# Experts' weights loaded in 8 KB runs, four tiles a step, with a seventh weight buffer

## The chip, the core and the metric

The kernel runs on one core of a Trainium2 chip. The metric is the device time of one execution in microseconds (us). The profile used here is of one further execution of the same program. Engines are named as in the profile: PE is the tensor engine's matmul, PEld its weight load, DVE the vector engine, ACT the scalar engine, POOL GpSimd, and SP the engine that issues nearly all loads, in the order of its program.

## What is computed

The network has two blocks, all in float32, for 256 tokens of 1024 features. The first block has two layers: attention with forget gates and then a mixture of experts; retention and then another mixture of experts. The second block, also of two layers, mixes tokens and a context of 256 rows (mLSTM, a gating unit, a convolution) and has dense feed-forward halves. The change lies in the mixture of experts, which is this:

```python
def hier_moe(h, wr_g, br_g, wr_e, br_e, w_gu, w_down):
    ...                                   # group of 8 experts by top-1, two experts in it by top-2
    return grouped_experts(xf, expert_id, gates, w_gu, w_down)

def grouped_experts(xf, expert_id, gates, w_gu, w_down):
    ...                                   # each token's row goes to its two experts e
    a, b = jnp.split(xb @ w_gu[e], 2, axis=-1)
    return (jax.nn.silu(a) * b) @ w_down[e]
    ...                                   # rows weighted by their gates, summed per token
```

There are 32 experts in each of the two layers. `w_gu[e]` is 1024 x 1024 (512 columns of gate, 512 of up; 4 MB), `w_down[e]` is 512 x 1024 (2 MB). So one layer reads 192 MB of experts' weights for 256 tokens.

## The kernel before

**Phases.** Attention runs from 0 to about 195 us of the profile, layer 0's experts from there to 760, retention to about 980, layer 1's experts from about 1000 to 1620, and the second block's own tail follows to the end. The second block's work on the context does not depend on the first block, so it is woven into the experts: `moe` is a generator that yields after each step, and at each yield the caller advances the *side work* by 0.8 of a step in layer 0 (the context's mixer, until about 607 us) and 0.88 in layer 1 (its feed-forward, then a mixer again). In layer 0 the experts run alone from there to 760 us.

**Experts.** A layer goes through eight groups q of four experts. Each expert has 32 places for tokens; the four experts' places are 128 rows of the products, and expert j uses columns 32 j to 32 j + 31 of the PE array, so four matmuls stand side by side. `gather(q)` (L895) puts the tokens of a group into `xg`, features on partitions, by products with the one-hot array `oh`; L173/`affine` multiplies by the gain column of each 128 features. The gate/up products (L956) go through eight chunks k of 128 features; each chunk has two halves of 512 columns and four experts: eight matmuls. Then ACT takes the silu (L965), DVE multiplies (L966), PE transposes the result `ha` (L969) into `hT`, and the down products (L976) go through four chunks k of 128 inner units, again eight matmuls each. A step, from yield to yield, is two chunks: sixteen matmuls. After the first two chunks of the down products the next group's gather and the transposes of its gates (`placed`, L923) are written; the result of group q - 1 is brought to the tokens (`combine`, L986) after chunk 3 of group q's gate/up products.

**Weights.** All large weights, the side work's too, go through tiles of 1 MB ([128, 2048] float32) from one pool `wp` of six places, taken in turn by `wt` (L126): a tile gets the place of the sixth tile before it, as soon as all its reads are done. At a layer's start three further places (`e0` to `e2`) are used first. Experts' tiles are loaded by `wload2` (L153), side weights by `wload` (L137), all issued by SP in program order; a load whose place is still in use holds up every load behind it. `pair(q, k)` loads chunk k of the four experts as two tiles of two experts: each partition holds one row of 1024 floats (4 KB) of each expert. So a chunk needs two tiles, and after its eight matmuls both are free. Group 7's down weights are loaded otherwise, in four quarters of the columns (1 KB runs, 0.5 MB each).

**The order around it.** At layer 0's start SP issues the first gate/up tiles, then small rows for the second block, and a load of the largest count of tokens per expert into a register (`cnti`, L1024). Before group 7 there is a branch on that count: an expert with more than 32 tokens would be computed densely there (`overflow`). The scheduler orders each engine's instructions by data dependence and program order; the sums over features are accumulated in PSUM.

Of the kernel before, what the change touches and what calls it, by code (L numbers as in the profile page):

```python
# [19 lines left out]
NEG = -1e30  # L20
RS = -8192.0                    # what rsqrt's scaled form carries
NE, CAP, FF = 32, 32, 512
R0, R1, R2, R3, R4 = 1.8, 0.8, 1.0, 0.88, 0.7           # steps of other work per step of the main path
AHEAD = 200                     # instructions that what the others wait for goes ahead of
TAPS = 6                        # convolution taps between other work
PIECE, WS = 512, 6              # elements per partition split at a time; pieces on chip
# [3 lines left out]
# columns of the constant array  # L30
C_ID, C_LE, C_LT, C_GE, C_ONE = 0, 128, 256, 384, 512
C_Z, C_LOW, C_UP = 640, 768, 896          # 0 where col <= row / col >= row, else NEG
C_IOTA, C_GRP, C_I8 = 1024, 1056, 1088
C_SEL, C_OFF = 1096, 1112                 # row 32 j + i, column i; rows of scales: what to add, 1 / RS
C_COS, C_SIN, C_RET = 1116, 1372, 1628         # rotary, decay
NCST = C_RET + 4 * 384

# modulation vectors: which third of the columns of w_mod, and which two of its quarters
# [4 lines left out]
def constants():  # L43
    """Tables that depend on shapes alone."""
# [35 lines left out]
class Tags:  # L80
    """A pool, some of whose tags lie in another one under other names."""
# [10 lines left out]
class Net:  # L92
    def __init__(self, tc, I, out, es):
# [8 lines left out]
        self.flip, self.extra = 0, []  # L102
        self.later, self.pending, self.taken = [], [], False
        self.early, self.hold = -99, None                  # pieces of weights whose low parts GpSimd makes

# [7 lines left out]
    def bank(self):  # L113
        """One bank, from the other pool while g's are taken."""
        return self.m()[:, 0:512] if self.taken else self.g()

    def two(self, mode, apart=False):
        """Two banks."""
# [7 lines left out]
    def wt(self, name):  # L126
        """A weight tile; some lie in the places of tiles that are no longer needed."""
        if self.extra:
            return self.pre.tile([P, 2048], F32, tag=self.extra.pop(0), name=name)
        return self.wp.tile([P, 2048], F32, tag="w", name=name)  # L130

    def wload(self, src):
        """One tile of weights: rows (k p) of src on the partitions."""
# [6 lines left out]
    def wtile(self):  # L140
        """A weight tile as [P, 2, D]."""
        return self.wt("w").rearrange("p (b d) -> p b d", b=2)

    def gain(self, src, g):
        """src [D] on all partitions."""
# [3 lines left out]
    def wload2(self, src):  # L149
        """The same rows of two experts: src [2, P, 1024]."""  # L150
        w = self.wt("w")
        v = w.rearrange("p (e c) -> p e c", e=2)
        self.nc.sync.dma_start(v, src.rearrange("e p c -> p e c"))  # L153
# [13 lines left out]
    def affine(self, o, i, scale, bias=None, eng=None):  # L167
        """o = i * scale + bias, per partition."""
# [10 lines left out]
    def split(self, pool, tag, src, shape=None, low=None):  # L179
        """src = H + L exactly, both in the tensor engine's one-pass format."""  # L180
# [12 lines left out]
    def wparts(self, w, mode):  # L193
        """Parts of a weight tile [P, k, c]: each a function of (row block, first column, last column)."""
# [15 lines left out]
    def pairs(self, a, b):  # L210
        """Products that make up a.b for operands in parts."""
        return [(a[0], b[0])] if len(a) == 1 else [(a[0], b[0]), (a[1], b[0]), (a[0], b[1])]

    def rstd(self, ss, n, eps=EPS):
        """1/sqrt(ss/n + eps)"""
# [4 lines left out]
    def rsqrt(self, h, scaled=False):  # L220
        """1/sqrt(h): a first guess from the exponent's bits, then Newton's steps. Scaled: RS times it, for one column."""
# [9 lines left out]
        for _ in range(3):  # L231
            if scaled:                  # y = c / sqrt(h) to (y h y - 3 c c) y = -2 c^3 / sqrt(h)
# [13 lines left out]
    def rms(self, x, b, junk, act=False):  # L246
        """rstd of token block b of x [P, 2, D]"""
# [12 lines left out]
    def transposed(self, xn, b, cb):  # L260
        """cb(k, psum [P, n, 128]) for the feature chunks k .. k + n of token block b of xn [P, 2, D]"""
# [1576 lines left out]
```

## Time and profile before

| | us |
|---|---|
| median of three runs | 2349.8 |
| the runs | 2347.91, 2349.8, 2354.22 |
| span of the profiled execution, first to last instruction | 2346.0 |
| what lies around the span, against the median | 3.8 |
| PE busy in the span | 2127.2 (91%) |
| VectorE busy | 1060.9 (45%) |
| mean granted clock of TensorE, share of full speed | 0.970 |
| loaded in the span | 686.64 MB, mean 293 GB/s |

The page divides the span into forty slices of 58.65 us and gives for each the busy tenths of each engine and of the DMA engines, PE's granted clock and the rate of transfer. The other views are of stretches of the span: busy time of each engine with the clock and the share of time in which the DMA engines were moving (the table by stretch), waits by what ended them, the queue's packets, and single instructions in order of time. The shares of a stretch are worth more here than those of the span, since phases have different limits.

### The profile page before, as it was taken

To read this page: it belongs to the slowest core of one execution; us is meant where nothing else is said; L and a number is where in the kernel's file an instruction comes from. 1 tells how busy PE (TensorE), PEld (TensorE's weight loads), DVE (VectorE), ACT (ScalarE), POOL (GpSimd) and SP (SyncE) were. 2 spreads that over 40 slices of the span, in tenths; PEclk is the share of its full clock that TensorE was granted. 3 is DMA by queue.
4 is the path that set the end of the run, shared out by engine and by line. 5 is a ranking of instruction groups with operands and counts; after the bars stand their busy time and mean duration, and the time that the engine had idled before them with its cause. 6 is when DMAs were issued, how large, how long until landed. Compare 5 with 4: busy or idle time off the path is not lost. (4 is left out here: it accounts for less than half of the span.)

```text
span 2346.0 us, 32803 instructions
## 1 busy us (share of the span) xinstructions
PE 2127.2 (91%) x12844; PEld 1433.4 (61%) x12845; DVE 1060.9 (45%) x2513; ACT 695.6 (30%) x1420; POOL 172.9 (7%) x194
## 2 busy tenths in 40 slices
PE   8998899889877999989899999987998998998998
PEld 7765445344222776855444444334787997787997
DVE  6556053322101766531121221415778556777555
ACT  4353111211000434520000000012555554554554
POOL 1001000000000111010000000001212002102000
PEclk9999999999988999989999999999999999999999
DMA  8864999999999977579999999999756554555551
GB/s 257 313 245 166 350 399 392 369 399 378 379 409 384 323 281 246 203 268 382 391 398 393 399 390 390 367 356 346 256 162 202 188 190 156 187 181 171 192 185 63
DMA packets 305320, 686.64 MB, mean 293 GB/s; under 512 B 22056, under 2 KB 163784, under 8 KB 298888
## 3 DMA queue, kind: packets, MB, share of 16 engines
q1 hardware_dynamic: 305096, 684.45, 79.9%
q8 instruction: 103, 1.69, 0.3%
q14 instruction: 57, 0.47, 0.1%
q10 hardware_dynamic: 64, 0.03, 0.0%
HBM read 681.78 MB, written 2.62 MB: 292 GB/s over the span
## 5 line engine op out<-in xcount | busy, mean ns | idle before, releaser
L190 DVE TENSOR_TENSOR wl<-w,wh 128x512 fp32r<-128x512 f32 x574 | 396.3, 707 | 252.4 <-ACT wh L185 233.7
L185 ACT CAST wh<-w 128x512 fp32r<-128x512 f32 x600 | 364.3, 621 | 355.5 <-PE psm L430 111.6
L956 PE MATMUL psm<-w,xg 128*32 128x512 f32 x2048 | 319.8, 632 | 61.8 <-DMA w<-in_expert_w_gu_dram 55.0
L430 PE MATMUL psg<-xt,w 128*128 128x256 f32 x1056 | 235.8, 381 | 20.5 <-DMA w<-in_w_gu_dram 11.3
L430 PEld LDWEIGHTS psg<-xt,w 128*128 128x128 f32 x1056 | 198.0, 190 | 71.1 <-issue 38.6
L956 PEld LDWEIGHTS psm<-w,xg 128*32 128x32 f32 x2048 | 66.4, 112 | 270.6 <-issue 150.4
L430 PE MATMUL psg<-xh,wh 128*128 128x256 f32 x608 | 177.2, 291 | 3.9 <-ACT wh L185 2.4
L430 PE MATMUL psm<-xh,wh 128*128 128x256 f32 x640 | 179.9, 281 | 0.6 <-ACT ffh L1450 0.6
L430 PE MATMUL psm<-xh,wl 128*128 128x256 f32 x640 | 179.8, 281 | 0.0
L430 PE MATMUL psm<-xl,wh 128*128 128x256 f32 x640 | 179.7, 281 | 0.0
L430 PE MATMUL psg<-xh,wl 128*128 128x256 f32 x608 | 175.1, 288 | 2.4 <-DVE wl L190 2.4
L430 PE MATMUL psg<-xl,wh 128*128 128x256 f32 x608 | 173.8, 286 | 0.0
L976 PE MATMUL psm<-w,hT 128*32 128x512 f32 (+1 forms) x1152 | 156.7, 564 | 16.0 <-DMA w<-in_expert_w_down_dram 12.5
L430 PEld LDWEIGHTS psg<-xh,wh 128*128 128x128 f32 x608 | 118.1, 194 | 18.6 <-ACT wh L185 9.5
L430 PEld LDWEIGHTS psm<-xh,wh 128*128 128x128 f32 x640 | 120.7, 189 | 1.9 <-ACT ffh L1450 1.1
L430 PEld LDWEIGHTS psm<-xh,wl 128*128 128x128 f32 x640 | 120.6, 188 | 0.7
L430 PEld LDWEIGHTS psg<-xh,wl 128*128 128x128 f32 x608 | 118.0, 194 | 4.9 <-DVE wl L190 4.2
L430 PEld LDWEIGHTS psm<-xl,wh 128*128 128x128 f32 x640 | 120.8, 189 | 0.0
L430 PEld LDWEIGHTS psg<-xl,wh 128*128 128x128 f32 x608 | 117.9, 194 | 0.3 <-issue 0.2
L965 ACT ACTIVATE ha<-psm 128x512 f32<-128x512 f32 x16 | 9.6, 597 | 334.3 <-PE psm L956 334.3
L988 DVE TENSOR_TENSOR x<-x,psg 128x512 f32<-128x512 f32 (+1 forms) x72 | 45.1, 628 | 123.2 <-PE psg L986 123.0
L976 PEld LDWEIGHTS psm<-w,hT 128*32 128x32 f32 x1152 | 38.6, 111 | 93.2 <-issue 52.2
(497 smaller groups left out, 3263.9 us busy)
## 6 DMA issues: line engine op xcount, KB each, us to landing
w<-in_expert_w_gu_dram SPq DMA_DIRECT2D x256, 1024.0 KB
w<-in_expert_w_down_dram SPq DMA_DIRECT2D x112, 1024.0 KB
w<-in_w_gu_dram SPq DMA_DIRECT2D x66, 1024.0 KB
w<-in_w_mod_dram SPq DMA_DIRECT2D x48, 1024.0 KB
w<-in_w_in_dram SPq DMA_DIRECT2D x40, 1024.0 KB
w<-in_w_down_dram SPq DMA_DIRECT2D x33, 1024.0 KB
w<-in_ret_w_in_dram SPq DMA_DIRECT2D x24, 1024.0 KB
w<-in_fox_w_in_dram SPq DMA_DIRECT2D x16, 1024.0 KB
```

Source lines behind the costliest of these rows:

```text
L185: nc.scalar.copy(h, src)
L190: eng.tensor_tensor(l, src, h.bitcast(F32), op=ALU.subtract)
L430: self.nc.tensor.matmul(o, a, x, start=i == 0, stop=i == len(mm) - 1)
L956: nc.tensor.matmul(gu[32 * j:32 * j + 32, half * 512:(half + 1) * 512], xg[:, k, 32 * j:32 * j + 32], ws[j // 2][:, j % 2, half * 512:(hal ...
L965: nc.scalar.activation(ha, gu[:, 0:512], AF.Silu)
L976: nc.tensor.matmul(o[32 * j:32 * j + 32, :], hT[:, k, 32 * j:32 * j + 32], w(j), start=k == 0, stop=k == 3)
L988: v.tensor_tensor(o, o, ps, op=ALU.add)
```

## The change

`wload2` loads 256 rows of one expert instead of 128 rows of two: partition p holds rows 2 p and 2 p + 1, which lie next to each other in memory, so each partition reads one run of 8 KB. A tile then holds two chunks of one expert: chunk 2 i has the even rows of a block of 256 features, chunk 2 i + 1 the odd ones. Four tiles, one for each expert, serve two chunks, and each is read until the second chunk's last half.

So that features and weights agree, the normalised tokens `xn` are written in that order of features (ACT reads x with a stride of two elements), and the gain's columns come in that order from a new small load, two transposes and a copy in the set-up (`pair_ffn`). The inner units are ordered likewise: the silu and the product read PSUM with a stride of two and write `ha` in the new order, except in group 7. `overflow` loads its gate/up weights in the new order. During `moe` a seventh place, from a pool `w7` of its own, joins the ring of `wp`'s six; afterwards the ring has six again. The loads ahead of the first step (`first`) are one set of four tiles, at the start (four before, too) and ahead of the branch (six before). Comments are gone too, and line numbers shift by 2 to 18.

```diff
     def wt(self, name):
         if self.extra:
             return self.pre.tile([P, 2048], F32, tag=self.extra.pop(0), name=name)
-        return self.wp.tile([P, 2048], F32, tag="w", name=name)
+        self.turn = (self.turn + 1) % len(self.ring)
+        return self.ring[self.turn].tile([P, 2048], F32, tag="w", name=name)
...
         w = self.wt("w")
-        v = w.rearrange("p (e c) -> p e c", e=2)
-        self.nc.sync.dma_start(v, src.rearrange("e p c -> p e c"))
+        v = w.rearrange("p (s c) -> p s c", s=2)
+        self.nc.sync.dma_start(v, src.rearrange("(p s) c -> p s c", s=2))
...
+        r3 = self.wt("rows3")[:8, :2 * P]
+        nc.sync.dma_start(r3, I["norm_ffn"].rearrange("l (k q) -> (l k) q", q=2 * P))
...
+        ps, pcol = self.g(), cp.tile([P, 16], F32, name="pcol")
+        for i in range(2):
+            nc.tensor.transpose(ps[:, i * 8:i * 8 + 8], r3.rearrange("r (p s) -> r s p", s=2)[:, i, :], self.ident[:8, :8])
+        nc.vector.tensor_copy(pcol.rearrange("p (r s) -> p s r", s=2), ps[:, :16].rearrange("p (s r) -> p s r", s=2))
+        self.vec["pair_ffn"] = pcol
...
-            pair = lambda q, k: [self.wload2(w_gu[4 * q + 2 * j:4 * q + 2 * j + 2, k * P:(k + 1) * P, :]) for j in range(2)]
+            self.ring = [self.wp] * 6 + [pool("w7", 1)]
+            quad = lambda q, k: [self.wload2(w_gu[4 * q + j, k * 256:(k + 1) * 256, :]) for j in range(4)]
             self.extra = ["e0", "e1", "e2"]
-            first = [pair(0, k) for k in range(2)]
-            gain = self.col("norm_ffn", l)
+            first = [quad(0, 0)]
+            gain = self.col("pair_ffn", l)
...
-                nc.scalar.activation(xn[:, b, :], x[:, b, :], AF.Copy, scale=rs[:, b:b + 1])
+                nc.scalar.activation(xn[:, b, :].rearrange("p (k s q) -> p k s q", k=4, s=2),
+                                     x[:, b, :].rearrange("p (k q s) -> p k s q", k=4, s=2), AF.Copy, scale=rs[:, b:b + 1])
...
-                    left, first = None, [pair(q, k) for k in range(3)]
+                    left, first = None, [quad(q, 0)]
...
-                    ws = first.pop(0) if first else pair(q, k)
+                    if k % 2 == 0:
+                        ws = first.pop(0) if first else quad(q, k // 2)
                     for half in range(2):
                         for j in range(4):
                             nc.tensor.matmul(gu[32 * j:32 * j + 32, half * 512:(half + 1) * 512],
                                              xg[:, k, 32 * j:32 * j + 32],
-                                             ws[j // 2][:, j % 2, half * 512:(half + 1) * 512], start=k == 0, stop=k == 7)
+                                             ws[j][:, k % 2, half * 512:(half + 1) * 512], start=k == 0, stop=k == 7)
...
-                nc.scalar.activation(ha, gu[:, 0:512], AF.Silu)
-                v.tensor_tensor(ha, ha, gu[:, 512:1024], op=ALU.mult)
+                order = lambda a: a if q == 7 else a.rearrange("p (k q s) -> p k s q", k=2, s=2)
+                ho = ha if q == 7 else ha.rearrange("p (k s q) -> p k s q", k=2, s=2)
+                nc.scalar.activation(ho, order(gu[:, 0:512]), AF.Silu)
+                v.tensor_tensor(ho, ho, order(gu[:, 512:1024]), op=ALU.mult)
...
-                        ws = [self.wload2(w_down[e0 + 2 * j:e0 + 2 * j + 2, k * P:(k + 1) * P, :]) for j in range(2)]
+                        if k % 2 == 0:
+                            ws = [self.wload2(w_down[e0 + j, k * P:(k + 2) * P, :]) for j in range(4)]
                         for half in range(2):
-                            down(k, y[:, half * 512:(half + 1) * 512], lambda j: ws[j // 2][:, j % 2, half * 512:(half + 1) * 512])
+                            down(k, y[:, half * 512:(half + 1) * 512], lambda j: ws[j][:, k % 2, half * 512:(half + 1) * 512])
...
+            self.ring = [self.wp] * 6
```

The scheduler's order shifts at three places. The first is PE in layer 1, where one group ends and the next group's tokens are gathered: `psg<-w,ffh` is a side product of the feed-forward, `psg<-cst,ha` the transposes of `ha`, `psg<-cst,og` those of the gates, `psg<-oh,xn` the gather and `psm<-w,hT` the down products. Before:

```order
L1416 MATMUL psg<-w,ffh 128x512 x8
L969 MATMUL psg<-cst,ha 128x128 x4
L923 MATMUL psg<-cst,og 128x128 x2
L895 MATMUL psg<-oh,xn 128x128 x2
L976 MATMUL psm<-w,hT 32x512 x10
L895 MATMUL psg<-oh,xn 128x128 x9
L976 MATMUL psm<-w,hT 32x512 x6
L895 MATMUL psg<-oh,xn 128x128 x5
L430 MATMUL psg<-xt,w 128x256 x16
```

The same place after:

```order
L1434 MATMUL psg<-w,ffh 128x512 x8
L985 MATMUL psg<-cst,ha 128x128 x4
L935 MATMUL psg<-cst,og 128x128 x2
L907 MATMUL psg<-oh,xn 128x128 x2
L992 MATMUL psm<-w,hT 32x512 x2
L907 MATMUL psg<-oh,xn 128x128 x3
L992 MATMUL psm<-w,hT 32x512
L907 MATMUL psg<-oh,xn 128x128 x11
L992 MATMUL psm<-w,hT 32x512 x13
L432 MATMUL psg<-xt,w 128x256 x16
```

All sixteen gather products now stand ahead of the last thirteen down products, where five of them stood behind the last down product before.

The second place is PE in layer 1 where a group's result is brought to the tokens: `psg<-ys,sgt` is `combine`, `psm<-w,xg` the next group's gate/up products, `psg<-xt,w` a side product. Before:

```order
L430 MATMUL psg<-xt,w 128x256 x16
L956 MATMUL psm<-w,xg 32x512 x8
L986 MATMUL psg<-ys,sgt 128x512
L956 MATMUL psm<-w,xg 32x512 x2
L986 MATMUL psg<-ys,sgt 128x512 x3
L956 MATMUL psm<-w,xg 32x512 x6
```

After:

```order
L432 MATMUL psg<-xt,w 128x256 x16
L969 MATMUL psm<-w,xg 32x512 x2
L1002 MATMUL psg<-ys,sgt 128x512 x2
L969 MATMUL psm<-w,xg 32x512
L1002 MATMUL psg<-ys,sgt 128x512 x2
L969 MATMUL psm<-w,xg 32x512 x13
L432 MATMUL psg<-xt,w 128x256 x16
```

The four products of `combine` stand behind the third of a step's sixteen matmuls now, and behind the eighth and tenth before.

The third place is SP at layer 0's start, from the last rows of attention's output weights on: `expert_w_gu` are experts' tiles, `w_in` a side tile, `gb`, `modr` and `rb` small rows, and TENSOR_LOAD takes the largest count into a register. Before:

```order
L137 DMA w<-in_fox_w_out_dram 128x4x512 x3
L153 DMA w<-in_expert_w_gu_dram 128x2x1024 x7
L554 DMA gb_5940<-in_b_in_dram 128x16
L1203 DMA modr_5993<-in_b_mod_dram 4x512 x2
L153 DMA w<-in_expert_w_gu_dram 128x2x1024
L1203 DMA modr_5993<-in_b_mod_dram 4x512 x4
```

After:

```order
L139 DMA w<-in_fox_w_out_dram 128x4x512 x3
L155 DMA w<-in_expert_w_gu_dram 128x2048 x8
L564 DMA gb_5951<-in_b_in_dram 128x16
L1221 DMA modr_6004<-in_b_mod_dram 4x512
L139 DMA w<-in_w_in_dram 128x4x512
L1221 DMA modr_6004<-in_b_mod_dram 4x512 x5
```

Eight experts' tiles stand in the first row instead of seven, and a side tile comes ahead of five of the small rows; one more experts' tile follows before the TENSOR_LOAD, where the side tile stood before.

## Rows read from the trace of the kernel before

**Rows 1.** The page, rate of transfer in forty slices of the span, GB/s.
```profile
GB/s 257 313 245 166 350 399 392 369 399 378 379 409 384 323 281 246 203 268 382 391 398 393 399 390 390 367 356 346 256 162 202 188 190 156 187 181 171 192 185 63
```

**Rows 2.** The page, loads by kind: count and size of each.
```profile
w<-in_expert_w_gu_dram SPq DMA_DIRECT2D x256, 1024.0 KB
w<-in_expert_w_down_dram SPq DMA_DIRECT2D x112, 1024.0 KB
```

**Rows 3.** By stretch: us; PE, PEld, DVE, ACT, POOL busy; PE clock, DMA share, GB/s.
```profile
411.00:469.00 58.00, 46.64 (x278) 19.66 (x279) 21.21 (x66) 11.59 (x44) 2.48 (x3) 0.94 0.93 368
620.00:760.00 140.00, 105.53 (x566) 31.96 (x560) 14.71 (x28) 8.76 (x19) 0.16 (x2) 0.88 1.03 399
1198.00:1281.00 83.00, 77.35 (x397) 41.22 (x395) 18.43 (x31) 3.90 (x9) 0.76 (x2) 1.00 1.03 397
```

**Rows 4.** Waits of PE, 1056 to 1466 us: total us, times, longest.
```profile
PE psm L956 <- DMA w<-in_expert_w_gu_dram: 11.6, 14, 1.6
```

**Rows 5.** DMA packets and queue share: 645 to 704, 70 to 73, 110 to 113 us.
```profile
DMA packets 6255, 24.14 MB, mean 409 GB/s; under 512 B 369, under 2 KB 369, under 8 KB 6253
q1 hardware_dynamic: 6253, 24.10, 102.2%
...
DMA packets 173, 1.29 MB, mean 429 GB/s; under 512 B 16, under 2 KB 16, under 8 KB 16
...
DMA packets 215, 1.27 MB, mean 424 GB/s; under 512 B 23, under 2 KB 65, under 8 KB 65
...
q1 hardware_dynamic: 215, 1.27, 104.1%
```

**Rows 6.** DMA rate in forty slices of 620 to 760 us, GB/s.
```profile
GB/s 412 411 405 410 405 412 412 408 407 407 408 408 410 411 411 411 408 407 411 408 405 411 410 411 398 415 387 383 403 411 412 410 408 412 380 348 349 348 347 348
```

**Rows 7.** Instructions by time, PE and SP near 655 us: start, us, instruction, [idle before].
```profile
655.33 1.91 PE L956 MATMUL psm<-w,xg 128*32 128x512 f32 x12 [1.50 <-DMA w<-in_expert_w_gu_dram]
656.46 1.19 SPq L153 DMA_DIRECT2D w<-in_expert_w_gu_dram  x2
```

**Rows 8.** Rate in slices of 600 to 700 us; SP and PE near 607 us.
```profile
GB/s 413 410 75 213 341 329 418 416 416 408 408 405 410 410 403 410 413 411 406 411 413 401 408 413 406 410 411 406 413 406 411 413 406 410 411 406 405 410 408 413
607.08 2.22 SPq L153 DMA_DIRECT2D w<-in_expert_w_gu_dram  x2
611.99 1.91 PE L956 MATMUL psm<-w,xg 128*32 128x512 f32 x12 [0.52 <-DMA w<-in_expert_w_gu_dram]
```

**Rows 9.** Instructions of PE by time, layer 1, a group's end and the next gather.
```profile
1210.36 7.10 PE L1416 MATMUL psg<-w,ffh 128*128 128x512 f32 x16 [0.73 <-DMA w<-in_w_down_dram]
1217.30 0.60 PE L969 MATMUL psg<-cst,ha 128*128 128x128 f32 x4
1217.73 0.38 PE L923 MATMUL psg<-cst,og 128*128 128x128 f32 x2
1217.95 0.61 PE L895 MATMUL psg<-oh,xn 128*128 128x128 f32 x4
...
1221.27 2.27 PE L895 MATMUL psg<-oh,xn 128*128 128x128 f32 x18
...
1225.32 1.38 PE L895 MATMUL psg<-oh,xn 128*128 128x128 f32 x10
```

**Rows 10.** Instructions of PE by time, layer 0, gate/up products and a combine.
```profile
577.38 3.64 PE L956 MATMUL psm<-w,xg 128*32 128x512 f32 x32
580.95 1.98 PE L986 MATMUL psg<-ys,sgt 128*128 128x512 f32 x4
...
585.76 1.92 PE L956 MATMUL psm<-w,xg 128*32 128x512 f32 x16
```

**Rows 11.** Instructions that write `ha` (230 to 760) and `xn` (180 to 260): ns min/median/max.
```profile
L965 ACT ACTIVATE ha<-psm x8: 597/597/598, 255.4 to 746.3; 128x512 f32<-128x512 f32 x8
L966 DVE TENSOR_TENSOR ha<-ha,psm x8: 679/687/689, 256.1 to 746.9; 128x512 f32<-128x512 f32 x8
L863 ACT ACTIVATE xn<-x,rs x2: 1133/1141/1149, 205.0 to 206.0; 128x1024 f32<-128x1024 f32 x2
```

More of the change, by code (lines that the diff above doesn't have):

```diff
@@ L102, in __init__ @@
         self.flip, self.extra = 0, []
+        self.ring, self.turn = [self.wp] * 6, 0
         self.later, self.pending, self.taken = [], [], False
@@ L1016, in moe, with load @@
                         yield
+            self.ring = [self.wp] * 6
     def overflow(self, l, mp, m2, xn, gov, cnti, gain):
         nc, I, x, v, tc = self.nc, self.I, self.x, self.nc.vector, self.tc
-        def load(src, e, kp):
-            nc.sync.dma_start(w, src[bass.ds(e, 1), kp * 256:(kp + 1) * 256, :].rearrange("o (k p) c -> p (o k) c", p=P))
+        def load(src, e, kp, order="o (k p) c -> p (o k) c"):
+            nc.sync.dma_start(w, src[bass.ds(e, 1), kp * 256:(kp + 1) * 256, :].rearrange(order, p=P))
             return w
@@ L1035, in overflow @@
                     for kp in range(4):
-                        w = load(I["expert_w_gu"][l], e, kp)
+                        w = load(I["expert_w_gu"][l], e, kp, "o (p k) c -> p (o k) c")
                         for b in range(2):
```

## The prediction

> **What bounds the kernel now.** I read the page's forty slices first [rows 1]: the rate of loading stands near 390 GB/s in slices 5 to 13 (layer 0's experts) and 18 to 28 (layer 1's), and far lower elsewhere. The loads by kind [rows 2] say what moves there: 256 + 112 tiles of 1 MB of experts' weights. Then the table by stretch [rows 3]. With the experts alone (620 to 760 us) the DMA share is 1.03 while PE is busy 105.53 of 140 us. In layer 1 beside the context's feed-forward (1198 to 1281) it is 1.03 again, but PE is busy 77.35 of 83 us: two resources full at once. In layer 0 beside the mLSTM (411 to 469) it is 0.93. The table of waits for layer 1 [rows 4] has landings at its head: PE lacks gate/up tiles fourteen times, 11.6 us in 410, never for more than 1.6. So in both expert stretches the queue of loads sets the pace, PE follows closely, and what the change can do is raise the rate of that queue or let it run empty.
>
> **The packets: a gain.** From 645 to 704 us nothing but expert tiles is loaded, in 4 KB runs (24.1 MB in 6253 packets): 409 GB/s at a queue share of 102.2% [rows 5]. So 1 MB (1.0486e6 bytes) takes 2.56 us. The trace has 8 KB runs too, those of the modulation weights: 70 to 73 us, 1.29 MB in 173 packets, 429 GB/s; 110 to 113 us, 424 GB/s at 104.1% [rows 5]. Between these lies 2.46 us a tile: 0.10 us less. Of the 368 tiles some ten a layer land before PE's expert work begins, so 348 x 0.10 = **34.8 us** of queue time go. The lower bound comes from the same rows divided by their shares: 409/102.2 = 4.00 GB/s per point of share, 424/104.1 = 4.07, so +1.8%, 0.045 us a tile, 15.7 us in all. The upper one is 429/409, +4.9%, 0.12 us a tile. I take 0.10, as the rates themselves give it, and keep 15.7 for a rival. The last group's down tiles stay in 1 KB runs (348 GB/s at the end of [rows 6]) and give nothing.
>
> The Trainium skill ("DMA: Bandwidth & Descriptors", section "Why small descriptors are slow (HBM only)") speaks against a gain of this size: it gives a fixed cost of about 3 cycles per packet on beats of 32 bytes. By that, 4 KB costs 128 + 3 cycles and 8 KB 256 + 3, 1.2% less per byte, an estimate of some 10 us in all. The rows of 8 KB packets show 3 to 5%, but over windows of 3 us only.
>
> **The ring: a loss.** Now a tile holds both chunks of one expert, a step (16 matmuls) needs four tiles, its first chunk already needs all four, and none is free before the second chunk is done. Before, two tiles served a chunk and were freed after 8 matmuls. The slack is worked out from three durations.
> - PE's side: the trace has two records for a matmul. Sixteen records of L956, two rounds over the four experts, last 1.92 us, 32 of them 3.64 [rows 10]: 0.95 us a round, 3.64 to 3.8 a step.
> - From release to issue: 0.18 us (the stretch from 655.33 ends its first round near 656.28, SP's entry stands at 656.46) [rows 7].
> - From issue to use: at 607 us the queue had run dry [rows 8]; a tile issued at 607.08 was first used at 611.99, 4.91 us later, of which 2.56 is transfer, so 2.35 us is fixed delay.
>
> After: let PE see a step's fourth tile at t = 0. Thirteen matmuls are left; three tiles come free near 2.85, the fourth at 3.8. A tile issued into the first free place is seen at 2.85 + 0.18 + 2.35 + 2.46 = 7.84. Three tiles are under way at t = 0 (seven places less four), so it is due as the fourth from then, at 4 x 2.46 = 9.84. Slack 2.0 us. Before, the like sum is 0.95 + 0.18 + 4.91 = 6.04 against five tiles, 12.8: slack 6.8. Where a side tile stands between (3.01 us at 348 GB/s [rows 6], 7.10 us of PE [rows 9]), the slack after is 2.55 us. So smooth running is still covered; a step in which PE is late by more is not. SP then holds a load that waits for a place, and behind it on SP every later load, the side work's too; on PE the matmul that waits for the fourth tile holds up the side products behind it.
>
> The steps that are late repeat with each group of four experts, and the rows of before price them [rows 9, 10]. A step with side work takes the queue 4 x 2.46 + 3.01 = 12.85 us, and PE 7.1 + 3.8 = 10.9.
> - The gather step adds four transposes of ha (0.60), two of the gates (0.38) and the gather's products (0.61 + 2.27 + 1.38 = 4.26); in the order of after all of these but none of the thirteen last down products stand ahead, and with the first three products (1.9 with the copies between) PE is at the thirteen about 18.0 us after the last step's fourth tile, 5.2 us after its own fourth landed. Over the slack: 5.2 - 2.55 = 2.6 us in which the queue runs dry. Before, the gather stood between down products that had freed tiles already. Between 0 (a step where PE was ahead) and 2.6 I take 2.0, nearer the top since [rows 3] shows no slack on PE in layer 1. Nine gathers lie beside side work (six in layer 1, three in layer 0): 18.
> - The combine step adds eight records of L986 (2 x 1.98): 10.9 + 0.95 + 3.96 + 0.95 = 16.8, late by 3.9, so up to 1.4 us dry. Between 0 and 1.4 I take 1.0; nine of them: 9.
> - Lateness shrinks by 12.85 - 10.9 = 2 us with each following step, so one does not add to the next.
> - Beside the mLSTM (share 0.93 [rows 3], waits on a chain, not on bytes) less slack costs between 0 and 6; I take 3.
> - Four gathers without side work: the step is 9.84 for the queue, PE 3.8 + 0.6 + 0.4 + 4.26 and the chain behind ha. L965 takes 597 ns and L966 687 [rows 11], now reading every second element of PSUM; at worst twice that. 0.6 to 1.9 us each, together 3.
>
> **The rest.** Order on SP: at layer 0's start nine gate/up tiles are issued ahead of the load of the counts (eight before), and one w_in tile goes earlier; ahead of the branch at group 7 four tiles stand instead of three. The queue carries the same bytes in either order; the seventh tile's memory may wait for fox's tiles: 0 to 5 us, I take 1. The normalised tokens are written in another order by L863 (two of 1141 ns [rows 11]), at worst doubled, on the path at each layer's start: 0 to 2.3 a layer, I take 0.5. The new 8-row load, two transposes and a copy lie in fox's first 100 us, whose rate is 257 GB/s [rows 1]: nothing; 2 if the ring is held. Instructions of POOL are unmoved.
>
> **Sum.** -34.8 + 18 + 9 + 3 + 3 + 2 = +0.2 us on a span of 2346.0; 3.8 us lie around it (median 2349.8): **2350**.
>
> **Rivals.**
> - *A, the forecast: the gaps eat the packets' gain.* Its own range is 2336 to 2363, from halves of the loss terms and their tops. For it: the share of 1.03 with PE busy 93% of 1198 to 1281 [rows 3], and PE's order at the gather.
> - *B, the ring is deep enough.* Seven places and work that PE does earlier than I place it; then only starts and the branch cost (some 5 us): 2349.8 - 34.8 + 5 = 2320, up to 2335 with a third of the gaps. For it: the tenths of DMA never fall below 9 in the pure stretch [rows 5], and PE's waits there are long, so lateness is rare; against it: layer 1.
> - *C, slower: four tiles freed together behind the gather and the combine.* Every gather at 2.6 and combine at 1.4 (36), the mLSTM stretch at 6, the four others at 1.9 (7.6), starts at 5: 54.6 - 34.8 = +20, 2370. It decides as soon as PE reaches the thirteen products more than 2.55 us after the fourth tile has landed, on each group, and if the strided reads push ha's chain beyond the side product's 7.10 us. Against it: it needs all of them at once.
> - *D, the longer packets give little.* 15.7 us instead of 34.8 with A's losses: 2349.8 + 0.2 + 19 = 2369. For it: the share's own division above. The Trainium skill's page named above would make it 10 us, 2375 by the same sum.
>
> **How the numbers follow.** Chances: A 0.44, B 0.32, C 0.15, D 0.09. A change under 0.3% (7 us) cannot be told from none here. A's range holds "same" at about 0.28, 0.06 faster, 0.10 slower; B is faster but for 0.02; C and D are slower by over 7 us. Faster 0.36, same 0.30, slower 0.34. Cases of both signs hold most of the chance, so the range runs from B's time to C's with its top terms: 2318 to 2377, beside A's own 2336 to 2363.
>
> **What would show it.** Packets of under 8 KB should fall by some 94,000; the pure stretch 645 to 704 should load at 424 to 429 GB/s (under 417: D). Each gather and combine in layer 1 should be followed by a gap of 1 to 2.6 us on the queue, with SP's next tile released by L976 or L956 and PE's wait for gate/up tiles grown from 11.6 us (A, C); a share that stays at 1.03 between 1121 and 1432 says B. Wrong would be all of it if PE's clock, 0.88 in the pure stretch [rows 3], falls in the longer waits for four tiles, or if the scheduler's order gives the late steps a different cover than these rows do.

## The result, and the profile after

The changed kernel takes 2385.91 us (median; 2382.63 to 2386.15) against 2351.69 before: a ratio of 1.0153, 95% interval 1.0138 to 1.0169. It is slower by 34 us where 2350 was forecast, and lies above the range's upper end of 2377.

The page of the changed kernel, span, rate in forty slices and packets, the first of which answer to [rows 1]:

```profile
span 2384.2 us, 32809 instructions
GB/s 262 304 255 160 356 351 373 335 381 394 389 370 380 366 234 246 248 207 388 371 398 376 385 391 395 349 358 350 272 170 186 191 192 164 180 192 168 179 193 62
DMA packets 258232, 686.65 MB, mean 288 GB/s; under 512 B 22064, under 2 KB 163800, under 8 KB 204696
```

The same bytes move in 47,088 fewer packets (305320 before), and the small ones fall by 94,192: the change does what it says. Yet the mean rate falls, most clearly in slices 6 to 8 (351, 373 and 335 where [rows 1] has 399, 392 and 369).

To see where the time went I take from each profiled execution the starts of the activation that writes `ha`, once per group. From the first to the sixth in layer 0 there is mostly side work, from the sixth to the eighth almost none.

| us | before | after | difference |
|---|---|---|---|
| to layer 0's first activation | 255.4 | 252.2 | -3.2 |
| first to sixth, layer 0 (mixed) | 366.7 | 384.9 | +18.2 |
| sixth to eighth, layer 0 (alone) | 124.1 | 131.6 | +7.5 |
| to layer 1's first | 305.7 | 310.4 | +4.7 |
| layer 1, first to eighth | 560.8 | 569.6 | +8.8 |
| to the end | 733.2 | 735.4 | +2.2 |

The expert stretches lose everywhere. The queue of the changed kernel from 645 to 704 us, in forty slices, answers to [rows 5]:

```profile
GB/s 439 422 400 317 372 411 422 422 411 433 294 361 267 411 428 411 433 417 422 411 422 433 444 405 283 394 417 383 417 411 433 294 39 233 400 417 422 417 417 439
DMA packets 3114, 22.75 MB, mean 386 GB/s; under 512 B 338, under 2 KB 338, under 8 KB 338
q1 hardware_dynamic: 3112, 22.73, 95.6%
```

While it flows it runs mostly at 411 to 439 GB/s, above the 409 of before; but it stumbles four times, near 649, 661, 680 and 692 us, once down to 39, and the mean falls to 386. The table by stretch (us; busy PE, PEld, DVE, ACT, POOL; clock, DMA share, GB/s) answers to [rows 3]:

```profile
638.00:770.00 132.00, 92.37 (x476) 27.86 (x476) 12.29 (x23) 6.48 (x14) 0.16 (x2) 0.91 0.95 379
1239.00:1318.00 79.00, 73.66 (x368) 36.35 (x366) 17.67 (x29) 4.55 (x11) 0.76 (x2) 1.00 0.97 384
```

The share is 0.95 and 0.97 in place of 1.03. PE's waits in layer 1 over the same work (1083 to 1501 us) answer to [rows 4]: 17.5 us for gate/up tiles instead of 11.6.

```profile
PE psm L969 <- DMA w<-in_expert_w_gu_dram: 17.5, 15, 2.5
PE psm L992 <- DMA w<-in_expert_w_down_dram: 3.8, 3, 2.5
```

These two are all of PE's waits for tiles that the view lists there. The kernel before has three more lines in its own (1056 to 1466 us), two of them for side tiles:

```profile
PE psg L430 <- DMA w<-in_w_gu_dram: 10.1, 11, 1.2
PE psg L1416 <- DMA w<-in_w_down_dram: 3.0, 4, 0.8
PE psm L976 <- DMA w<-in_expert_w_down_dram: 2.0, 2, 1.6
```

So all waits of PE for tiles fall, from 26.7 to 21.3 us, though the stretch gets longer. What grows is PE's busy time. From the first to the eighth activation of layer 1, before and then after:

```profile
1052.00:1612.80 560.80, 516.64 (x2707) 268.22 (x2707) 140.87 (x298) 43.30 (x97) 12.46 (x16) 0.99 1.00 384
1079.20:1648.80 569.60, 534.23 (x2708) 274.38 (x2708) 139.43 (x300) 42.55 (x96) 12.89 (x18) 0.99 0.96 377
```

PE is busy 17.6 us longer with the same products, at the same clock. The next rows show how that can be: a product whose tile comes alone takes PE 1.04 us (x2, since a product has two records), where [rows 10] has four products side by side in 0.91 (x32 in 3.64). A late tile thus shows as busy time too, and not only as a wait. No run separates the two.

How a dry moment comes about is best seen where experts run alone. PE and SP of the changed kernel in order of time (start, us, instruction, [idle before]):

```profile
670.88 1.04 PE L969 MATMUL psm<-w,xg 128*32 128x512 f32 x2 [1.35 <-DMA w<-in_expert_w_gu_dram]
673.36 1.04 PE L969 MATMUL psm<-w,xg 128*32 128x512 f32 x2 [1.44 <-DMA w<-in_expert_w_gu_dram]
675.85 6.01 PE L969 MATMUL psm<-w,xg 128*32 128x512 f32 x30 [1.44 <-DMA w<-in_expert_w_gu_dram]
683.29 1.04 PE L969 MATMUL psm<-w,xg 128*32 128x512 f32 x2 [1.44 <-DMA w<-in_expert_w_gu_dram]
687.74 5.97 PE L969 MATMUL psm<-w,xg 128*32 128x512 f32 x30 [3.40 <-DMA w<-in_expert_w_gu_dram]
...
692.76 0.33 SPq L155 DMA_DIRECT2D w<-in_expert_w_gu_dram  x1
693.18 1.47 SPq L155 DMA_DIRECT2D w<-in_expert_w_down_dram  x3
...
695.15 1.04 PE L969 MATMUL psm<-w,xg 128*32 128x512 f32 x2 [1.44 <-DMA w<-in_expert_w_gu_dram]
700.20 2.79 PE L969 MATMUL psm<-w,xg 128*32 128x512 f32 x12 [4.00 <-DMA w<-in_expert_w_gu_dram]
```

Each wait ends on a tile: 670.88, 673.36, 675.85, so tiles come 2.48 to 2.49 us apart while the queue flows. At 687.74 a step's fourth tile is there. Only at 692.76, 5.02 us later, does SP issue the next load, and then four within 1.4 us: all four places came free together. The first of these tiles is used at 700.20, 7.44 us after its issue. This step takes 12.46 us, not 4 x 2.48 = 9.9. Not every step does: from 636 to 758 us the first load of each four is issued 9.8 to 12.8 us after that of the four before.

The trace records sixteen landing signals for a tile. For the tile issued at 692.76 fifteen came from 697.10 to 697.45 and the last at 700.15; for the one of [rows 8], issued at 607.08, all came from 611.40 to 611.95. The first came 4.3 us after the issue in both, so most of the difference between 4.91 and 7.44 us is the last signal, which came late. Why it trails is not shown.

### The profile page after: what moved, and what is told of

The parts are those of the page before. It is cut to its first block, busy times and chain, and to the rows that moved or that the text cites. A ratio compares the mean times of both kernels' runs of the same rounds, so it can differ in the third digit from the quotient of the medians.

```text
span 2384.2 us, 32809 instructions
## 1 busy us (share of the span) xinstructions
PE 2163.7 (91%) x12846; PEld 1446.1 (61%) x12847; DVE 1058.3 (44%) x2514; ACT 695.1 (29%) x1420; POOL 173.1 (7%) x194
## 5 line engine op out<-in xcount | busy, mean ns | idle before, releaser
L969 PE MATMUL psm<-w,xg 128*32 128x512 f32 x2048 | 342.5, 643 | 85.3 <-DMA w<-in_expert_w_gu_dram 79.6
L969 PEld LDWEIGHTS psm<-w,xg 128*32 128x32 f32 x2048 | 76.5, 116 | 305.8 <-issue 169.9
L992 PE MATMUL psm<-w,hT 128*32 128x512 f32 (+1 forms) x1152 | 178.8, 587 | 27.7 <-DMA w<-in_expert_w_down_dram 23.7
L982 DVE TENSOR_TENSOR ha<-ha,psm 128x512 f32<-128x512 f32 x16 | 11.0, 686 | 196.9 <-ACT ha L981 160.9
```

The lines of the kernel that those rows point to most:

```text
L969: nc.tensor.matmul(gu[32 * j:32 * j + 32, half * 512:(half + 1) * 512], xg[:, k, 32 * j:32 * j + 32], ws[j][:, k % 2, half * 512:(half + 1 ...
L982: v.tensor_tensor(ho, ho, order(gu[:, 512:1024]), op=ALU.mult)
L992: nc.tensor.matmul(o[32 * j:32 * j + 32, :], hT[:, k, 32 * j:32 * j + 32], w(j), start=k == 0, stop=k == 3)
```

## The experiments

All ratios are to runs of the kernel before on the same chip (medians 2348 to 2352 us). "L", "R" and the other letters are theories named in the expectations.

**An eighth buffer.** `ha` and `hT` have one place each to make room.

```diff
-            self.ring = [self.wp] * 6 + [pool("w7", 1)]
+            self.ring = [self.wp] * 6 + [pool("w7", 2)] * 2
```

> The changed kernel with an eighth weight buffer in the experts (the tiles ha and hT get one place instead of two to make room); all else as changed. Theory L (the loop of four tiles freed together): in the changed kernel's trace the fourth tile is seen at 687.74, the next tile is issued at 692.76 and used at 700.20, 12.4 us for a step, against 4 x 2.48 = 9.9 us of queue; one more buffer gives the queue 5 x 2.48 = 12.4 us, so smooth steps stop running dry and the gather and combine steps lose 2.5 us less each: 2325 to 2342 us, and PE's wait for gate/up tiles falls from 79.6 us to under 45. Rival R (the 8 KB runs or the strided reads themselves delay landings and products): the buffer changes nothing, 2378 to 2388.

Measured 2325.92 us, 0.9886 (0.9859 to 0.9912). From the changed kernel this is -60 us by one buffer: the short ring was the cost, and R falls. PE's wait for gate/up tiles fell from 79.6 to 51.2 us, less far than expected. The queue of this kernel from 645 to 704 us no longer stumbles:

```profile
GB/s 422 433 422 422 411 433 422 411 422 428 417 411 433 428 417 411 433 428 417 411 433 417 428 383 439 428 389 361 428 422 417 417 433 428 394 400 411 433 428 411
DMA packets 3380, 24.68 MB, mean 418 GB/s; under 512 B 371, under 2 KB 371, under 8 KB 371
```

**4 KB runs, all else as changed.** The order of rows, tokens, gains and inner units is before's.

```diff
-        self.nc.sync.dma_start(v, src.rearrange("(p s) c -> p s c", s=2))
+        self.nc.sync.dma_start(v, src.rearrange("(s p) c -> p s c", s=2))
```

> The changed kernel's tiles (two chunks of one expert), steps of four tiles and seven buffers, but rows loaded in before's order, so in 4 KB runs, with no strided read. Theory L: the dry loop stays at some 12.4 us a step where it sets the pace, and 0.07 us a tile is lost where the queue flows: 2392 to 2408 us. Rival R: the long runs or strides are the cost, so the time falls to 2345 to 2365.

Measured 2388.02 us, 1.0162 (1.0138 to 1.0186). Not told apart from the changed kernel: with a queue that runs dry the longer runs bring nothing that can be measured, and they are not the harm either. Over the three expert stretches of the table (mixed, alone, layer 1) the DMA share is 0.96, 0.99 and 0.98 with 4 KB runs and 0.93, 0.95 and 0.96 with 8 KB runs: what the longer runs save comes back as an idle queue. R falls; L had put it 4 us higher at least.

**The gather and combine split over two steps each.**

```diff
-                    if k == 3 and left:
-                        for half in range(2):
-                            left(half)
+                    if k in (3, 5) and left:
+                        left(k // 2 - 1)
...
                             (xg, steps), sgt = gather(q + 1), placed(q + 1)
-                            for _ in steps:
-                                pass
+                        if k % 2:
+                            next(steps)
```

> The changed kernel with the gather written in two halves, one in each down step, and the two halves of combine in two gate/up steps, so that no step of PE carries more than about 2.5 us of it. Theory G (the queue runs dry behind the gather and combine steps): the gaps of 2 to 3.5 us there mostly vanish, 20 to 30 us in both layers together: 2355 to 2367 us. Rival L alone (smooth steps run dry too): 2368 to 2382. Rival R: 2380 to 2388.

Measured 2375.7 us, 1.0116 (1.0084 to 1.0148). Layer 1 (first to eighth activation) falls from 569.6 to 558.7 us, layer 0's mixed stretch rises from 384.9 to 392.3. So splitting the late steps gives back 11 us in layer 1, but not in layer 0, and most of the loss is elsewhere, as L alone expected.

**Pairs of experts one after the other, groups 6 and 7 of layer 0.** Of a step, all products of experts 0 and 1 come first (`js` is (0, 1), then (2, 3)).

```diff
-                        for j in range(4):
-                            nc.tensor.matmul(gu[32 * j:32 * j + 32, half * 512:(half + 1) * 512],
+                                for j in js:
+                                    nc.tensor.matmul(gu[32 * j:32 * j + 32, half * 512:(half + 1) * 512],
```

> The changed kernel, where in groups 6 and 7 of layer 0 (no side work) a step's products go expert pair by expert pair: all of experts 0 and 1 first, then all of 2 and 3, so two tiles are freed half a step earlier; PE takes two products side by side there instead of four, some 7.6 us a step instead of 3.8. Theory L: the steps of that stretch return to 4 x 2.48 = 9.9 us, some 10 us less in all: 2373 to 2379 us. Theory 'PE's pace matters there': slower than 2386 by 5 to 15. Rival R: 2383 to 2388.

Measured 2379.39 us, 1.0132 (1.0109 to 1.0156), and the stretch from the sixth to the eighth activation falls from 131.6 to 122.2 us, as L expected, though PE does the same products at half the parallelism. In all the run is just above L's range and, by the intervals, not told apart from the changed kernel. PE's clock rises as well (0.97 from 638 to 770 us, 0.91 in the changed kernel), so the gain of that stretch is not the earlier release alone; the filler run below shows what the clock is worth by itself.

**The kernel before with eight, five, seven and four buffers.** Here the ring of `moe` alone differs (outside it there are six).

```diff
-        return self.wp.tile([P, 2048], F32, tag="w", name=name)
+        self.turn = (self.turn + 1) % len(self.ring)
+        return self.ring[self.turn].tile([P, 2048], F32, tag="w", name=name)
...
+            self.ring = [self.wp] * 6 + [pool("w7", 2)] * 2
```

> The kernel before (4 KB runs, two tiles a chunk) with eight weight buffers in the experts, ha and hT in one place each. Theory L with a gain of 0.07 us a tile from the longer runs: this kernel's queue is hardly ever dry (in its trace the tiles land 2.56 us apart, with some 43 us above that in both layers), so buffers alone bring little: 2335 to 2352 us. Rival B (buffers are all that the eight-buffer version of the changed kernel gained): 2320 to 2332.

Measured 2315.66 us, 0.9857 (0.9838 to 0.9877): the fastest of all, a miss for L, and below the rival's range too. With eight buffers the kernel before is 10 us faster than the changed one (2325.92).

> The kernel before with five weight buffers in the experts instead of six. Theory L (what counts is how early a place comes free, not the number alone): first product to reuse 0.95 + 0.18 + 7.4 us = 8.5 against 4 x 2.56 = 10.2 us, so smooth steps stay covered and only late steps lose: 2355 to 2385 us. Rival 'the number of places decides': over 2395, as the changed kernel with seven places for four tiles a step is at 2386.

Measured 2422.06 us, 1.0316 (1.0295 to 1.0338): a miss for L again, and on the rival's side. Before was short of buffers itself.

> The kernel before with the change's seventh buffer alone. Theory D (the depth of the ring sets the time in the stretches with side work, and 6 to 8 buffers gave 34 us): 2322 to 2336 us, so the seventh buffer alone is a gain and the four-tile steps cost 50 us and more. Theory of the prediction (before's queue has 6.8 us of slack): 2346 to 2353.

Measured 2324.4 us, 0.9900 (0.9883 to 0.9916). The change's seventh buffer alone gains 24 us. So, taken in this order, the change splits up: the buffer -24 (2348 to 2324), tiles of one expert, four a step, +64 (to 2388.0; 62 by the ratios), the longer runs -2 (to 2385.9, within the noise). The parts depend on each other: with eight buffers the four-tile step costs 17 us (2315.66 to 2332.45 below).

Where the buffers count is seen by stretch. From the sixth to the eighth activation, where the experts run alone, before's order takes 124.6 us with five buffers, 124.1 with six, 125.3 with seven and 124.3 with eight. In layer 1, beside the side work, it takes 591.9, 560.8, 548.8 and 547.5.

**Eight buffers and 4 KB runs.** The edits of the first two experiments together.

> The changed kernel with eight buffers (2325.9 us measured), but with 4 KB runs and no strided read. Theory L: with the queue seldom dry each of some 340 tiles pays 0.07 us again, 24 us: 2342 to 2354. Rival N (the longer runs bring nothing, as the seven-buffer pair 2385.9 and 2388.0 suggests): 2322 to 2332.

Measured 2332.45 us, 0.9927 (0.9904 to 0.9949): just above N's range. Against 2325.92 the longer runs give 6.5 us where the queue is mostly full, not 24: the profiles have 3.9 in layer 0's mixed stretch, 2.7 alone (122.9 to 120.2) and 3.4 in layer 1 (553.8 to 550.4), and lose 3 behind the experts. In layer 1 the eight-buffer kernel with long runs keeps PE busy for 443.96 of 460 us (1060 to 1520 us) at a DMA share of 0.99; before with eight needs 433.22 for as many products, and its queue is the fuller one; before itself stands last:

```profile
1060.00:1520.00 460.00, 443.96 (x2223) 226.84 (x2222) 115.78 (x199) 29.63 (x70) 7.48 (x12) 0.99 0.99 395
...
1060.00:1520.00 460.00, 433.22 (x2223) 221.04 (x2221) 115.75 (x198) 29.73 (x70) 7.49 (x12) 1.00 1.02 393
...
1060.00:1520.00 460.00, 427.01 (x2210) 220.73 (x2209) 114.82 (x198) 30.34 (x73) 8.05 (x13) 1.00 1.02 390
```

**Six buffers in the changed kernel**, `self.ring = [self.wp] * 6`.

> The changed kernel with six buffers instead of seven. Theory L: the queue has 3 x 2.48 = 7.4 us ahead of a loop of some 12.4 us, so nearly each of 92 steps loses up to 2.5 us more than with seven: 2440 to 2600 us. Rival S (only the late steps, gather and combine, cost): some 32 of them by 2.5 us: 2430 to 2470. Rival R: 2380 to 2395.

Measured 2487.36 us, 1.0579 (1.0553 to 1.0606): L's range, above S's. The queue from 645 to 704 us comes nearly to a stop in most steps:

```profile
GB/s 387 369 389 422 433 439 422 428 405 156 161 422 200 311 417 444 439 439 422 306 44 239 428 417 417 417 433 422 72 228 433 405 439 422 433 428 22 156 433 417
```

**Filler products to hold the clock.** `fill` is twelve transposes of the third tile.

```diff
+                            if l == 0 and q >= 6 and k % 2 == 0 and half == 0 and j == 3:
+                                fill(ws[2])
                             nc.tensor.matmul(gu[32 * j:32 * j + 32, half * 512:(half + 1) * 512],
```

> The changed kernel with twelve extra transposes of a step's third tile between the third and the fourth tile's first products, in groups 6 and 7 of layer 0, where there is no side work; their results are not used. Theory K (after waits of up to 4 us PE's clock is at half speed, the thirteen products take 4.5 to 6.4 us instead of 3.6, and so the places come free late): the time from the activation of group 5 to that of group 7, 131.6 us in the changed kernel, falls to 119 to 125, the whole to 2372 to 2379. Rival (the landing after issue alone, 7.4 us, makes the gap): 130 to 135 us there and 2383 to 2390 in all.

Measured 2382.7 us, 1.0144 (1.0127 to 1.0161); the stretch takes 128.8 us, between both. The fillers (L944) do quicken the thirteen products, to 3.62 us:

```profile
696.40 2.22 PE L944 MATMUL psg<-cst,w 128*128 128x128 f32 x12
698.55 3.62 PE L976 MATMUL psm<-w,xg 128*32 128x512 f32 x26
```

and the mean granted clock from 638 to 770 us is 0.95 instead of 0.91 (a share of the upper of the two levels, 2.4 GHz). But only 3 us come of it there, so K falls as the main cause.

**Eight buffers and the split gather.** Both edits from above.

> The changed kernel with eight buffers and the gather and combine each split over two steps. Theory PE (with eight buffers PE is busy 444 of 460 us from 1060 to 1520, so layer 1 is bound by PE): no gain there, 2316 to 2328 us. Theory G (gaps behind gather and combine are still what is lost): 2306 to 2316.

Measured 2322.18 us, 0.9897 (0.9881 to 0.9913). Layer 1 does fall by 6.8 us (550.4 to 543.6), which theory PE did not expect: PE was not the only limit there. And the mixed stretch of layer 0 rises by 3.8; in all the run cannot be told from 2325.92.

**Experts 2 and 3 one chunk behind.** In chunk k experts 0 and 1 use chunk k, experts 2 and 3 chunk k - 1, so a chunk needs and frees two tiles.

```diff
+                            kk = k - j // 2
+                            if 0 <= kk < 8:
...
-                                             ws[j][:, k % 2, half * 512:(half + 1) * 512], start=k == 0, stop=k == 7)
+                                                 ws[j][:, kk % 2, half * 512:(half + 1) * 512], start=kk == 0, stop=kk == 7)
```

> The changed kernel (8 KB runs, seven buffers, tiles of one expert's two chunks), but experts 2 and 3 run one chunk behind experts 0 and 1 in the gate/up and down products, so that each chunk needs two new tiles and frees two, as before; the price is two rounds in each of 30 phases with two products side by side instead of four, up to 1.9 us of PE each. Theory D (what the four-tile step costs is the depth it takes from the ring): near the seven-buffer kernel of before's arrangement (2324.4 measured), less 2 to 6 us for the longer runs, plus 5 to 30 for PE's price: 2325 to 2350. Rival (the cost lies in the one-expert tiles or the long runs, not in the four tiles a step): 2372 to 2390.

Measured 2395.04 us, 1.0195 (1.0166 to 1.0224): the theory's range was missed by 45 us, and the rival's by 5. Where the experts run alone the new order does what it was made for (131.6 to 122.6 us); layer 1 loses 22 (569.6 to 591.6). It frees two tiles a chunk, but always holds four, and now the side products wait for tiles (PE, layer 1): between 1299.63 and 1313.14 us SP issues no load at all.

```profile
1302.41 8.83 PE L432 MATMUL psg<-xt,w 128*128 128x256 f32 x32 [3.59 <-DMA w<-in_w_gu_dram]
...
1318.67 7.14 PE L432 MATMUL psg<-xt,w 128*128 128x256 f32 x32 [2.14 <-DMA w<-in_w_gu_dram]
```

From this came theory H, that what counts is the buffers beyond those in use. It was put to two runs.

> The kernel with experts 2 and 3 one chunk behind (2395.0 us with seven buffers), now with eight buffers. Theory H, made after that miss: what counts is the number of buffers beyond those that the products in progress hold, two in before's arrangement and four here and in the changed kernel. By the runs so far: two beyond 2487 us; three 2386, 2388, 2395, 2422; four 2326, 2332, 2350; five 2324; six 2316. Eight buffers leave four beyond: 2326 to 2352. Rival Q (the kernel with lagging experts is slow by PE's price for rounds with two products): 2380 to 2395.

Measured 2343.48 us, 0.9974 (0.9963 to 0.9985): H's range; PE's price (Q) is not the main cause.

> The kernel before with four weight buffers in the experts. Theory H: two beyond the two in use, as in the changed kernel with six (2487.4 us): 2470 to 2550. Rival (the four-tile step has a cost of its own, so that before's arrangement at the same depth is well below it): 2430 to 2460.

Measured 2583.35 us, 1.0979 (1.0951 to 1.1007): beyond both ranges. H orders the runs but does not give their size:

| buffers beyond those in use | before's order, two in use | four tiles a step, four in use | experts 2, 3 behind, four in use |
|---|---|---|---|
| 2 | 2583 (4 buffers) | 2487 (6) | |
| 3 | 2422 (5) | 2386 (7), 2388 in 4 KB runs | 2395 (7) |
| 4 | 2350 (6) | 2326 (8), 2332 in 4 KB runs | 2343 (8) |
| 5 | 2324 (7) | | |
| 6 | 2316 (8) | | |

Each further buffer gains in every column. At the same count the four-tile step is not slower than before's order but faster; by this count its harm at seven buffers is the two that it takes out of the ring. The count was made after most of these runs, it leaves out the places that side tiles hold, and it does not show PE's longer busy time as a cost of its own.

## Why the prediction was wrong, point by point

The sum had the packets at -34.8 us, the gaps behind the four-tile steps at +33, the small terms at +2 and the seventh buffer at nothing. The runs, one part after the other, give -2 for the packets, +64 for the four-tile steps with the small terms, and -24 for the buffer.

**The packets.** 0.10 us a tile was taken; it is 0.07 to 0.08, 2.56 against 2.48 to 2.49 (the row at 673.36). The two windows of [rows 5] were short, and read high; rival D's bound, 0.045, was too low. The estimate of 1.2% worked out from the Trainium skill ("DMA: Bandwidth & Descriptors", "Why small descriptors are slow (HBM only)") does not agree with these 3%. More important, 34.8 us was the wrong kind of number: it multiplies all tiles by a gain that counts only where the queue sets the end. With seven buffers it was worth 2 us within the noise, with eight 6.5.

**The slack after, 2.0 us: the step that failed.** From it the prediction concluded that smooth running is still covered, and counted only late steps. Both of its terms were too small. Three tiles were to be free at 2.85 us and the fourth at 3.8; but each of the four is read in the last round of products, so they come free together: 5.02 us from the fourth tile's first product to the next issue at 692.76. From 687.74 to 692.55 the granted clock is 0.53, so mostly at the lower level of 1.2 GHz; with the fillers the thirteen products took 3.62 us. From issue to use 2.35 + 2.46 = 4.81 us was taken, and 7.44 is seen. That makes 12.46 us against 9.84 for this step. So steps with neither gather nor combine ran dry too, and a dry queue has no use for faster packets. One buffer more, which gives the queue one more tile to load meanwhile, takes off 60 us. The prediction also named a falling clock as a sign of being wrong; it falls within such a step, but not over the stretch (0.91 from 638 to 770 us, 0.88 before), and the fillers gave back only 3 us.

**The slack of before, 6.8 us.** This erred the other way: it made the seventh buffer worth nothing, where the kernel before with seven takes 24 us less and with eight 34. For experts alone the slack is real, as the stretch of 124 us with five to eight buffers shows. It is missing beside the side work, and [rows 8] hold a case. The rate falls to 75 GB/s there: PE was at side products until 606.98, and SP, whose last load dates from 600.22, issued the next only at 607.08:

```profile
593.59 13.47 PE L1390 MATMUL psg<-w,yT 128*128 128x512 f32 x31
```

The prediction took from these rows the time from issue to use, and no loss. It also took the share of 1.03 in [rows 3] to mean that the queue sets the pace in both expert stretches; in those two windows it did. From the first to the eighth activation of layer 1 the share is 1.00 before and 1.02 with seven buffers, and in layer 0's mixed part likewise; two hundredths of 560 us are 11 of the 12 us that layer 1 gained.

**PE's products.** A round of products stood at 0.95 us, for four experts at once. That tiles which come one by one make PE take their products alone, 1.04 us each, was not in the sum. In layer 1, from the first to the eighth activation, PE is busy 510.99 us in before's order with seven buffers and 536.38 in the four-tile order (both in 4 KB runs): 25.4 us more, where the time grows by 24.5. A deeper ring lets tiles come earlier and so acts on this too (525.57 with eight buffers); how the 64 us divide between PE and the queue stays open.

**The gather and combine.** This term was right in kind. Behind the gather's thirteen products PE waits 2.51 us in layer 1 (the bound was 2.6):

```profile
1253.25 3.63 PE L992 MATMUL psm<-w,hT 128*32 128x512 f32 x30
1257.30 1.04 PE L992 MATMUL psm<-w,hT 128*32 128x512 f32 x2 [0.42 <-DMA w<-in_expert_w_down_dram]
1260.85 3.62 PE L992 MATMUL psm<-w,hT 128*32 128x512 f32 x26 [2.51 <-DMA w<-in_expert_w_down_dram]
```

The whole loss of four tiles a step, 64 us from seven buffers in before's order to seven in the new one (both in 4 KB runs), stood in the sum as 18 + 9 + 3 + 3 = 33. By stretch: 33.6 us in layer 0's mixed part (352.4 to 386.1), where three gathers, three combines and 3 us for the mLSTM were counted, some 12; 24.5 in layer 1 (548.8 to 573.3), where six of each, 18 us, were counted.

**Layer 0's part.** Why the mixed stretch of layer 0 loses so much more than layer 1 is not settled. Before with eight buffers is 17.6 us shorter there (366.7 to 349.1), so it was short of depth from the start; that alone does not explain the size.

**The small terms.** The strided reads cost nothing in `ha` (597 and 686 ns, as [rows 11]) and 57 ns each in `xn`; the start came 3.2 us earlier, not 1.5 later. Ahead of the branch at group 7 four tiles stand instead of six, not instead of three. A's own range is not what its words give: halves of the 33 us with the 2 lead to 2334, their tops with the 2 to 2367.

```profile
L981 ACT ACTIVATE ha<-psm x8: 597/597/598, 252.2 to 768.8; 128x512 f32<-128x512 f32 x8
L982 DVE TENSOR_TENSOR ha<-ha,psm x8: 677/686/689, 252.9 to 769.4; 128x512 f32<-128x512 f32 x8
...
L874 ACT ACTIVATE xn<-x,rs x2: 1189/1198/1207, 199.5 to 200.6; 128x1024 f32<-128x1024 f32 x2
```

**The rivals.** C named the mechanism, four tiles freed together, but priced it at 2370 and put it at 0.15, since it counted only late steps. B fails on its condition: seven places were not deep enough; with eight the kernel comes to B's time (2326 of 2320 to 2335). D's forecast of a short gain held in part, for another reason: its sign, under 417 GB/s from 645 to 704 us, came true with 386, but through the gaps and not through slow packets.

## What to carry to other kernels

Count the buffers of a ring that loads can use while the products in progress hold theirs; a change of tile or step that doubles the held ones needs as many more buffers before its gain can show. A DMA share near 1 over a stretch is no proof that more depth brings nothing: compare it with the share of a stretch in which the queue is known to be full (1.02 to 1.03 here), and try one buffer more, alone, before making the transfers faster. Look at an engine's busy time for the same work as well as at its waits. And of a change with several parts, price each part alone against the kernel before.

## What the runs showed of the hardware

The time from the issue of 1 MB to its use was 4.91 us at 607.08 in the kernel before and 7.44 us at 692.76 in the changed one; the first of the sixteen landing signals came after 4.3 us in both, and the last after 4.87 and 7.39. A product that uses 32 columns of the array takes 1.04 us alone (the rows x2 above), and thirteen to sixteen, four side by side, 3.62 to 3.64. Runs of 8 KB moved 1 MB in 2.48 to 2.49 us and 418 GB/s over a full stretch (eight buffers, 645 to 704 us), where 4 KB runs took 2.56 us and moved at 409. Over 4.8 us of products that followed a wait of 3.40 us the granted clock was 0.53.
